# Feed-forward weights at 64, 96 and 160 bytes from the input, modulo 256, instead of 32

## The chip, the core and the metric

The kernel runs on one core of a Trainium2 chip (trn2). The metric is the device time of one execution in microseconds (us); the time before is the median of three runs. One further execution was taken with the hardware profiler; its lines are what this document quotes. In them PE is TensorE (matmuls), PEld is its loading of weights, DVE is VectorE, ACT is ScalarE, POOL is GpSimd and SP is SyncE. L154 is line 154 of the kernel before.

## The reference

One block of a decoder on 512 positions of 1024 channels, in float32. The part that matters here is its second half, the feed-forward with a gate, whose 2816 inner channels pass a short causal convolution:

```python
x = x + mix @ w_o[l]
h = rmsnorm(x, norm2_g[l])
gu = h @ w_ffn_in[l]
g = causal_dwconv(gu[..., :D_FF], ffn_conv_w[l]) + ffn_conv_b[l]
x = x + (jax.nn.silu(g) * gu[..., D_FF:]) @ w_ffn_out[l]
```

Ahead of it stand the input projections, a sparse attention with three branches, a short convolution, two merge gates and the output projection `w_o`.

## The kernel before, in words

All activations lie with channels on the 128 partitions and positions along the row. Every float32 product is made of three matmuls in the type `float32r`: the operands are split into a high part and the rest, and high x high, high x low and low x high are summed in PSUM. `dense` (L149 to L162) issues them, one unit of three matmuls per 128 channels of the contraction: L154 (weights high, input high), L157 (weights high, input low), and L159 or, where all low weights come last, L161 (weights low, input high). Each matmul has its own load of 128 x 128 weights, and the load for the next one runs while the input of the present one streams.

The feed-forward input product `h @ w_ffn_in` is made by a fast matrix product with seven multiplications in place of eight. For two tiles of 128 output channels (`f`, `f + 1`), `n` = 0 (gate) or 1 (up), the weights form a 2 x 2 block matrix, of which seven blocks or sums of blocks ("forms") are needed, and likewise seven sums of the input, which are made once. There are 11 values of `f` and 2 of `n`, so 22 passes. The forms are:

- `a11` and `a12`, in the tiles `wh` and `wl` (`form_a1`, L956). For a few passes the low part is made by a DMA that adds, in tile `dl` (`lo_by_dma`, L967).
- 3 and 2, a pair: one tile `sh` (high) and one `sl` (low) of 2 x 512 columns each; and 4 and 1, a second pair in tiles of the same kind (`forms_s`, L976). DVE makes the sums (L991 to L996), and `put` (L982) splits them with one ACT and one DVE instruction. The tags `sh` and `sl` have four buffers each (`NSQ`), used in turn: the pairs of two passes.
- `a22`, in the tiles `th` and `tl` (`form_a22`, L999).

The input's sums lie in `xf_h` and `xf_l` (L1061, L1062), four tiles of channels by seven sums by 256 columns: two halves of the 512 positions. `ff_pair` (L1127) issues the seven products of a pass, each over four tiles of channels with 256 columns streaming, 12 matmuls a product. Between passes stand down products (`down_products`, L1210), 512 columns wide, whose weights are in `wh`, `wl` or `dl`; the last few are 256 wide.

Where a tile lies in a partition's memory is decided by pools. `px` and `pf` lie on the left side, one behind the other; `pw`, with the pairs and `a22`, grows from the right end downward, and so does `pc` below it, which holds `mix_h` and `mix_l`, the input of the `w_o` product (L1089 to L1101; 8 output tiles of 24 matmuls, 512 columns wide). Padding tiles fix the addresses: `xf_pad` of `XF_PAD` = 8 words ahead of `xf_h`, and `pf_pad` of `PF_PAD` = 48 words, which brings what follows in `pf` back to its place. The addresses of the built program, modulo 256 bytes, are: the parts of `wh`, `wl`, `dl` that hold weights, `sh`, `sl`, `th`, `tl`, `ah`, `al`, `mix_h` and `mix_l` at 224, `xf_h` and `xf_l` at 0. So the feed-forward weights lie 32 bytes ahead of (below) their input, and the weights of the down products and of `w_o` at the same place as theirs.

In the token projection (`tok_products`, L235, and `first_products`, L252) roles are different: the activations `xg_h` and `xg_l` are the loaded operand, at 224, and chunks of 350, 350 and 348 columns of weights (`th`, `wh_t`, `tok_lo`) stream from many different addresses. In the attention's scores (L732, L733) the keys `kk` stream, from 224 or 96, and the queries `qT`, at 224 or 96 too, are loaded.

The order of all instructions is fixed by a scheduler when the program is built.

Of the kernel before, what the change touches and what calls it, by code (L numbers as in the profile page):

```python
# [11 lines left out]
F32 = mybir.dt.float32  # L12
F32R = mybir.dt.float32r
# [5 lines left out]
P = 128  # L19
# [22 lines left out]
C_G = C_V + 256  # L42
TOKC = C_G + 24
LINE = 256
XF_PAD = 8
PF_PAD = 48
NW4 = 5
NWR = 3
NE = 3
# [15 lines left out]
NSQ = 4  # L65
# [29 lines left out]
def tile_block(ctx: ExitStack, tc: tile.TileContext, xT, pos, par, par2, w_tok, w_a3, w_gate, w_ao, w_bo, w_o,  # L95
# [12 lines left out]
    def const(shape, name, dt=F32, pool=sb):  # L108
        return pool.tile(shape, dt, name=name, tag=name)
# [827 lines left out]
    pw = ctx.enter_context(tc.tile_pool(name="pw", bufs=1, side="right"))  # L937
# [8 lines left out]
    def split(h, l, v):  # L946
        m = nc.scalar.activation(h, v, AF.Copy)  # L947
        nc.vector.tensor_sub(l, v, h.bitcast(F32))  # L948
        return m
# [17 lines left out]
    def lo_by_dma(name, raw, src, view=lambda t: t, after=None):  # L967
# [5 lines left out]
        nc.gpsimd.dma_start(view(l), src, accum_op=ALU.add)  # L973
        return l

    def forms_s(f, n, raws, form):  # L976
        nm = f"{n}_{f}"
        a11, a12 = raws[0][:, 0:half], raws[0][:, half:D]
        a21, a22 = raws[1][:, 0:half], raws[1][:, half:D]
        q = lambda name, tag, dt, bufs: pw.tile([P, 2, half], dt, name=f"{name}{nm}", tag=tag, bufs=bufs)  # L980

        def put(names, v):  # L982
            h, l = (q(f"s{x}{names[0]}", f"s{x}", F32R, NSQ) for x in "hl")
            m = split(h, l, v)
            if names[0] == 4:
                ends["sh"] = m
            for i, name in enumerate(names):
                form[name] = (h[:, i], l[:, i])

        s = q("s32", "sf", F32, NSF)  # L990
        nc.vector.tensor_sub(s[:, 0], a11, a21)  # L991
        nc.vector.tensor_sub(s[:, 1], a22, s[:, 0])  # L992
        put((3, 2), s)
        s4 = q("s41", "sf", F32, NSF)
        nc.vector.tensor_sub(s4[:, 0], a12, s[:, 1])
        nc.vector.tensor_add(s4[:, 1], a21, a22)  # L996
        put((4, 1), s4)
# [11 lines left out]
    def ff_forms(f, n):  # L1009

        form = {}
        raws = [ff_raw(f, n, m) for m in range(2)]
        form_a1(f, n, raws[0], form)
        forms_s(f, n, raws, form)
        form_a22(f, n, raws[1], form)
        return form
# [5 lines left out]
    def first_sums(n):  # L1022
        forms_s(0, n, [ff_raw(0, n, m) for m in range(2)], first_form[n])
# [35 lines left out]

    const([P, XF_PAD], "xf_pad", F32, px)  # L1060
    xf_h = const([P, 4, 7, TH], "xf_h", F32R, px)  # L1061
# [48 lines left out]
    for i in range(NU):  # L1110
        u = const([P, 2, S + 2], f"c{i}", F32, pf)
        nc.gpsimd.memset(u[:, :, 0:2], 0.0)
        u_bufs.append(u)
    const([P, PF_PAD], "pf_pad", F32, pf)
    a_hl = {}
# [196 lines left out]
```

## Time and profile before

| | |
|---|---|
| time, median of three runs | 716.25 us (716.16 to 717.05) |
| time of the profiled execution | 716.42 us |
| its span, first to last instruction | 714.5 us |
| PE busy | 709.0 us (99%) |
| PEld busy | 635.7 us (89%) |
| DVE busy | 574.1 us (80%) |
| ACT busy | 415.5 us (58%) |
| POOL busy | 127.3 us (18%) |
| matmuls in the trace | 4275 |

A matmul's row gives the time from its start to the modelled end of its result; successive matmuls overlap, so that the sum of durations is longer than the busy time of PE. What a matmul costs in a row of matmuls is the time from its start to the start of the next, called a step here. A group's row reads: line, engine, operation, out<-in, partitions x elements, count, then busy us and mean ns of one, then idle time ahead of it.

### The profile page before, as it was taken

The page shows a single profiled execution, that of the slowest core. Times are in us where ns is not written, and L with a number is a line of the kernel's source. Part 1 is how long each engine was busy: PE and PEld are TensorE (multiplying, and loading weights), DVE is VectorE, ACT ScalarE, POOL GpSimd, SP SyncE. Part 2 cuts the span into 40 slices and gives each one's busy share as a digit, 9 for nine tenths or more (in the row PEclk, how much of TensorE's full clock was granted, in tenths as well). Part 3 has the DMA queues.
Part 4 walks back from the last instruction along what each step waited for, and adds up shares of the span by engine and source line. Part 5 has one row for each costly group of instructions (what it writes and reads, how often), then busy time and mean ns, then how long its engine had stood idle before and what let it go on. Part 6 is the DMA issues. An engine that isn't in the chain of part 4 may idle for free.

```text
span 714.5 us, 11190 instructions
## 1 busy us (share of the span) xinstructions
PE 709.0 (99%) x4275; PEld 635.7 (89%) x4275; DVE 574.1 (80%) x988; ACT 415.5 (58%) x706; POOL 127.3 (18%) x111
## 2 busy tenths in 40 slices
PE   9999999999999999999999999999999999999997
PEld 8999888888888888888889999999999999999986
DVE  7978978785566784788876999899898998989833
ACT  7776566777767875444665665555455554455320
POOL 1122443343333311232002011010000010000000
PEclk9999999999999999999999999999999999999999
DMA  8633552121111122246447476645655556552413
GB/s 297 228 89 100 159 126 73 47 90 59 60 60 59 60 64 84 91 146 202 181 133 163 118 170 165 167 120 124 174 145 129 138 124 161 129 148 89 118 30 117
DMA packets 36804, 88.19 MB, mean 123 GB/s; under 512 B 7440, under 2 KB 10896, under 8 KB 36752
## 3 DMA queue, kind: packets, MB, share of 16 engines
q1 hardware_dynamic: 30672, 74.42, 32.8%
q0 software_dynamic: 5648, 12.58, 10.8%
q8 instruction: 33, 0.54, 0.3%
q10 hardware_dynamic: 432, 0.49, 0.2%
q14 instruction: 19, 0.16, 0.1%
HBM read 85.39 MB, written 2.10 MB: 122 GB/s over the span
## 4 chain that ended last, share of the span: by engine, by line
PE 92%; issue 4%; DMA 2%; DVE 1%; POOL 0%; ACT 0%; POOLq 0%; SPq 0%; DVEq 0%
PE p L154 8%; PE p L161 8%; PE p L157 8%; PE pdn L157 4%; PE pdn L154 4%; PE pg L159 4%; PE pg L157 4%; PE pg L154 4%; PE pdn L161 4%; PE pa L154 3%; PE pa L157 3%; PE pt L810 2%; PE po L161 2%; PE po L157 2%; PE po L154 2%
## 5 line engine op out<-in xcount | busy, mean ns | idle before, releaser
L154 PE MATMUL p<-xf_h,sh 128*128 128x256 f32 x352 | 86.4, 280 | 0.0
L157 PE MATMUL p<-xf_l,sh 128*128 128x256 f32 x352 | 86.0, 278 | 0.0
L154 PEld LDWEIGHTS p<-xf_h,sh 128*128 128x128 f32 x352 | 66.5, 189 | 0.1
L157 PEld LDWEIGHTS p<-xf_l,sh 128*128 128x128 f32 x352 | 65.9, 187 | 0.0
L947 ACT ACTIVATE sh<-s 128x1024 fp32r<-128x1024 f32 x44 | 45.7, 1050 | 19.0 <-DVE s L992 15.7
L973 POOL DMA_DIRECT2D wl_d<-in_w_dn_dram x16 | 19.1, 1195 | 204.0 <-ACT wl_d L970 204.0
L948 DVE TENSOR_TENSOR sl<-s,sh 128x1024 fp32r<-128x1024 f32 x44 | 53.1, 1216 | 2.8 <-ACT sh L947 2.7
L161 PE MATMUL p<-xf_h,sl 128*128 128x256 f32 x352 | 54.9, 279 | 0.0
L157 PE MATMUL pdn<-al,wh_d 128*128 128x512 f32 x134 | 52.4, 391 | 0.0
L154 PE MATMUL pdn<-ah,wh_d 128*128 128x512 f32 x134 | 52.0, 390 | 0.0
L159 PE MATMUL pg<-xg_h,wl_g 128*128 128x512 f32 x128 | 50.5, 395 | 0.0
L157 PE MATMUL pg<-xg_l,wh_g 128*128 128x512 f32 x128 | 50.3, 393 | 0.0
L154 PE MATMUL pg<-xg_h,wh_g 128*128 128x512 f32 x128 | 50.3, 393 | 0.0
L161 PEld LDWEIGHTS p<-xf_h,sl 128*128 128x128 f32 x352 | 47.4, 188 | 0.3
L154 PE MATMUL p<-xf_h,wh_s 128*128 128x256 f32 x176 | 43.3, 280 | 0.0
L157 PE MATMUL p<-xf_l,wh_s 128*128 128x256 f32 x176 | 43.1, 278 | 0.0
L761 ACT ACTIVATE e<-sc,mx 128x512 f32<-128x512 f32 (+3 forms) x64 | 33.2, 521 | 16.5 <-DVE mx L760 14.7
L154 PE MATMUL pa<-xg_h,wh_a 128*128 128x512 f32 x96 | 37.9, 395 | 0.0
L157 PE MATMUL pa<-xg_l,wh_a 128*128 128x512 f32 x96 | 37.6, 392 | 0.0
L787 ACT ACTIVATE e<-e,sums 128x512 f32<-128x512 f32 (+3 forms) x64 | 30.7, 552 | 8.2 <-DVE sums L737 8.0
L814 DVE TENSOR_TENSOR pl<-pt,ph 128x512 fp32r<-128x512 f32 x40 | 27.1, 683 | 10.2 <-ACT ph L813 10.0
L161 PE MATMUL pdn<-ah,wl_d 128*128 128x512 f32 x128 | 34.2, 389 | 0.0
(361 smaller groups left out, 2111.5 us busy)
## 6 DMA issues: line engine op xcount, KB each, us to landing
wr_s<-in_w_ff_dram SPq DMA_DIRECT2D x44, 512.0 KB, 3.8
wr_d<-in_w_dn_dram SPq DMA_DIRECT2D x22, 512.0 KB, 3.7
wr_g<-in_w_gate_dram SPq DMA_DIRECT2D x16, 512.0 KB, 3.5
wl_d<-in_w_dn_dram POOLq DMA_DIRECT2D x16, 512.0 KB, 6.6
wr_a<-in_w_a_dram SPq DMA_DIRECT2D x12, 512.0 KB, 3.7
wr_t<-in_w_tok_dram SPq DMA_DIRECT2D x10, 524.0 KB, 6.2
wr_o<-in_w_o_dram SPq DMA_DIRECT2D x8, 512.0 KB, 3.8
wr_ao<-in_w_ao_dram SPq DMA_DIRECT2D x4, 512.0 KB, 3.4
```

The source lines that it names most:

```text
L154: m = nc.tensor.matmul(acc, wh, xh, start=first and i == 0, stop=False)
L157: nc.tensor.matmul(acc, wh, xl, start=False, stop=False)
L159: m = nc.tensor.matmul(acc, wl, xh, start=False, stop=last and i == n - 1)
L161: m = nc.tensor.matmul(acc, wl, xh, start=False, stop=last and i == n - 1)
L761: nc.scalar.activation(e[:, i, 0:nk], sc[:, o:o + nk], AF.Exp, bias=mx[:, i], accum_out=sums[:, i])
L787: nc.scalar.activation(v, v, AF.Copy, scale=sums[:, i])
L810: ends["pt"] = nc.tensor.transpose(pt[:, i * P:(i + 1) * P], e[:, i, kt * P:(kt + 1) * P], ident)
L814: m = nc.vector.tensor_sub(pl, pt, ph.bitcast(F32))
L947: m = nc.scalar.activation(h, v, AF.Copy)
L948: nc.vector.tensor_sub(l, v, h.bitcast(F32))
L973: nc.gpsimd.dma_start(view(l), src, accum_op=ALU.add)
```

## The change

`XF_PAD` goes from 8 to 40 words, which moves `xf_h` and `xf_l` up by 128 bytes, and `PF_PAD` from 48 to 16, which keeps what follows in place. The tags `sh` and `sl` are divided into `sh3`, `sl3` (forms 3 and 2) and `sh4`, `sl4` (forms 4 and 1), with two buffers each instead of four for both. At the first use of each pair a padding tile is made: 56 words under the first pair's, 48 under the second's.

```diff
-XF_PAD = 8
-PF_PAD = 48
+XF_PAD = 40
+PF_PAD = 16
+S32_PAD, S41_PAD = 56, 48
...
+    pads = {3: [], 4: []}
+
     def forms_s(f, n, raws, form):
...
         def put(names, v):
-            h, l = (q(f"s{x}{names[0]}", f"s{x}", F32R, NSQ) for x in "hl")
+            h, l = (q(f"s{x}{names[0]}", f"s{x}{names[0]}", F32R, NSQ // 2) for x in "hl")
             m = split(h, l, v)
+            if not pads[names[0]]:
+                pads[names[0]].append(const([P, S32_PAD if names[0] == 3 else S41_PAD], f"pad{names[0]}", F32, pw))
```

The addresses of the built program, modulo 256 bytes, before and after:

| tiles | before | after |
|---|---|---|
| `xf_h`, `xf_l` | 0 | 128 |
| `sh`, `sl` of forms 3 and 2 | 224 | 64 |
| `sh`, `sl` of forms 4 and 1 | 224 | 32 |
| weights in `wh`, `wl`, `dl`, `th`, `tl` | 224 | 224 |
| `mix_h`, `mix_l` | 224 | 64 |
| `ah`, `al` | 224 | 224 |

Measured downward from the input, the weights are at 64 (forms 3, 2), 96 (forms 4, 1) and 160 bytes (`a11`, `a12`, `a22`).

## The prediction

> **What bounds the kernel now.** I read the page first, then the busy time by stretches, then the groups of matmuls by tile and shape, and last the timeline of single matmuls. The page:
>
> ```profile
> span 714.5 us, 11190 instructions
> ...
> PE 709.0 (99%) x4275; PEld 635.7 (89%) x4275; DVE 574.1 (80%) x988; ACT 415.5 (58%) x706; POOL 127.3 (18%) x111
> ...
> PE 92%; issue 4%; DMA 2%; DVE 1%; POOL 0%; ACT 0%; POOLq 0%; SPq 0%; DVEq 0%
> ```
>
> PE is busy for 709.0 of 714.5 us, and 92% of the chain that ended last is PE. So a nanosecond more or less on one matmul is a nanosecond of the kernel, as long as no other engine comes up behind it. The stretches show whether one does (first the stage of the output projection `w_o`, then the feed-forward):
>
> ```profile
> 328.70:372.30 43.60, 43.60 (x194) 36.15 (x193) 33.64 (x51) 27.24 (x40) 4.43 (x3) 1.00 0.56 175
> 372.30:677.60 305.30, 304.74 (x2244) 289.04 (x2244) 277.23 (x372) 162.49 (x203) 25.09 (x23) 1.00 0.56 139
> ```
>
> The columns are length, then busy time of PE, PEld, DVE, ACT and POOL, the granted clock, and the DMA share. In the feed-forward stretch PE has no idle time to speak of (304.74 of 305.30), the clock is 1.00, and DVE, which makes the weights' forms, has 277.23, so 28 us of slack. A gain of a few us on PE stays covered.
>
> **The unit of the sum: one 256-wide step.** In each pass of the feed-forward (22 of them) the seven products have 4 units of 3 matmuls, 84 in all: 24 with forms 3 and 2, 24 with forms 4 and 1, 36 with the other three. That is 528, 528 and 792, together 1848. One pass in the timeline, its first row and the first row after it:
>
> ```profile
> 612.24 0.28 PE L154 MATMUL p<-xf_h,wh_s 128*128 128x256 f32 x1
> ...
> 622.04 0.39 PE L154 MATMUL pdn<-ah,wh_d 128*128 128x512 f32 x1
> ```
>
> (622.04 - 612.24) / 84 = 116.7 ns from start to start; 1848 such steps are 215.7 us. The pipelined matmul itself lasts longer; its duration by groups, here for a pair's high and low parts:
>
> ```profile
> L154 PE MATMUL p<-xf_h,sh 128*128 128x256 f32 x341 | 83.5, 280 | 0.0
> L157 PE MATMUL p<-xf_l,sh 128*128 128x256 f32 x341 | 83.3, 278 | 0.0
> L161 PE MATMUL p<-xf_h,sl 128*128 128x256 f32 x341 | 53.2, 279 | 0.0
> ```
>
> The mean is 279 ns, so step = duration - 162 ns. Durations can thus be compared where the timeline's 10 ns are too coarse.
>
> **The change, part by part.** It removes, adds and moves no instruction: rows and waits of all five engines are the same in both programs. Tiles `s`, `s4`, `sh`, `sl` still have as many buffers (two for each pair, taken in turn, as four taken in turn by two pairs gave), so no wait for a buffer changes. Only addresses change. I call "ahead" the input's address minus that of the weights loaded while it streams, modulo 256 bytes. It goes from 32 everywhere to 64 (forms 3, 2), 96 (forms 4, 1) and 160 (the others). One thing moves that the change doesn't speak of: `mix_h` and `mix_l`, which lie below the pair tiles, go from 224 to 64 modulo 256, and the 192 matmuls of `w_o` (8 tiles of 24) from 0 to 96 ahead (64 - 224 is -160, or 96 modulo 256).
>
> Does the distance cost anything? Before has other distances in other places. Distance 0, at the same width of 256, in the last down products:
>
> ```profile
> L157 PE MATMUL pdn_e<-al,wh_d 128*128 128x256 f32 x12 | 3.3, 283 | 0.0
> L154 PE MATMUL pdn_e<-ah,wh_d 128*128 128x256 f32 x12 | 3.3, 282 | 0.0
> L159 PE MATMUL pdn_e<-ah,wl_d 128*128 128x256 f32 x12 | 3.2, 282 | 0.0
> ...
> 698.03 0.28 PE L157 MATMUL pdn_e<-al,wh_d 128*128 128x256 f32 x1
> ...
> 698.87 0.28 PE L154 MATMUL pdn_e<-ah,wh_d 128*128 128x256 f32 x1
> ```
>
> Seven steps in 0.84 us are 120 ns, 3.3 more than at 32 ahead, and the durations say the same (282 to 283 against 279). Distance 128, width 256, in two score products of the attention, each a pair of rows:
>
> ```profile
> L732 PE MATMUL sc<-kk,qT 128*128 128x256 f32 x1 | 0.3, 279 | 0.0
> L733 PE MATMUL sc<-kk,qT 128*128 128x256 f32 x1 | 0.3, 279 | 0.0
> ...
> L733 PE MATMUL sc<-kk,qT 128*128 128x256 f32 x1 | 0.3, 282 | 0.0
> L732 PE MATMUL sc<-kk,qT 128*128 128x256 f32 x1 | 0.3, 276 | 0.0
> ```
>
> Mean 279, as at 32 ahead; 276 is the shortest that I find at this width. The new distances themselves occur only in the token projection, where 350 columns stream. There, pairs of matmuls on one chunk of weights, two pairs each in the order 0 ahead, 32 ahead, 160 ahead, 96 ahead:
>
> ```profile
> L242 PE MATMUL pj_t<-wh_t,xg_l 128*128 128x350 f32 x1 | 0.3, 323 | 0.0
> L239 PE MATMUL pj_t<-wh_t,xg_h 128*128 128x350 f32 x1 | 0.3, 322 | 0.0
> L239 PE MATMUL pj_s<-wh_t,xg_h 128*128 128x350 f32 x1 | 0.3, 323 | 0.0
> L242 PE MATMUL pj_s<-wh_t,xg_l 128*128 128x350 f32 x1 | 0.3, 318 | 0.0
> ...
> L239 PE MATMUL pj_t<-th,xg_h 128*128 128x350 f32 x1 | 0.3, 322 | 0.0
> L242 PE MATMUL pj_t<-th,xg_l 128*128 128x350 f32 x1 | 0.3, 321 | 0.0
> L239 PE MATMUL pj_s<-th,xg_h 128*128 128x350 f32 x1 | 0.3, 320 | 0.0
> L242 PE MATMUL pj_s<-th,xg_l 128*128 128x350 f32 x1 | 0.3, 320 | 0.0
> ...
> L242 PE MATMUL pj_s<-wh_t,xg_l 128*128 128x350 f32 x1 | 0.3, 326 | 0.0
> L239 PE MATMUL pj_s<-wh_t,xg_h 128*128 128x350 f32 x1 | 0.3, 321 | 0.0
> L239 PE MATMUL pj_t<-wh_t,xg_h 128*128 128x350 f32 x1 | 0.3, 325 | 0.0
> L242 PE MATMUL pj_t<-wh_t,xg_l 128*128 128x350 f32 x1 | 0.3, 323 | 0.0
> ...
> L242 PE MATMUL pj_t<-th,xg_l 128*128 128x350 f32 x1 | 0.3, 327 | 0.0
> L239 PE MATMUL pj_t<-th,xg_h 128*128 128x350 f32 x1 | 0.3, 322 | 0.0
> L239 PE MATMUL pj_s<-th,xg_h 128*128 128x350 f32 x1 | 0.3, 322 | 0.0
> L242 PE MATMUL pj_s<-th,xg_l 128*128 128x350 f32 x1 | 0.3, 322 | 0.0
> ```
>
> Means 321.5, 320.75, 323.75 and 323.25. So at this width 160 ahead costs 3.0 ns over 32 ahead, and 96 ahead 2.5. But 0 and 32 differ by less than 1 ns there, against 3.5 at width 256: where 350 columns stream the distance acts otherwise, and a row of the same width counts more for me.
>
> Term by term, from rows of width 256 first:
> - Forms 3 and 2, 64 ahead. From 0 to 32 bytes the duration fell by 3.5 ns. Another 32 bytes on the same slope go to the shortest row, 276, that is -3 ns. Bounds: -3 (that row) and +3.5 (the row at 0). I take -3: 528 x -3 = -1.6 us.
> - Forms 4 and 1, 96 ahead. Between 64 ahead (-3 by the slope) and 128 ahead (0 by the score rows); the token rows say +2.5. Bounds -3 and +3.5. I take half the gain, -1.5: 528 x -1.5 = -0.8 us.
> - Other forms, 160 ahead. The nearest row of the width is 128 ahead, 279: nothing. The token rows say +3. Bounds -3 and +3.5. I take 0.
> - `w_o`, 0 to 96 ahead, width 512:
>
> ```profile
> L154 PE MATMUL po<-mix_h,wh_o 128*128 128x512 f32 x64 | 24.7, 389 | 0.0
> ```
>
> No row of this width shows another distance within one stage. The token rows give 323.25 - 321.5 = +1.75 from 0 to 96; the bounds are -3.5 (what 0 to 32 gave at width 256) and +3.5. I take +1.75: 192 x 1.75 = +0.3 us.
>
> Sum: -1.6 - 0.8 + 0 + 0.3 = -2.1 us. The profiled execution took 716.42 us (span 714.5 and 1.9 around it), the median of the runs is 716.25, so the two agree within 0.2. 716.4 - 2.1 = 714.3 us.
>
> A rule of the Trainium skill speaks against this change. The page "TensorE: Matmul & The Clock Gate", in "Step-by-step: what each phase is for", says that TensorE reads the streaming operand and the next weights through two independent ports, so that loading the next weights takes nothing from the running matmul. By that rule distance couldn't matter and the time would stay. The 282 to 283 ns against 279 of the same shape speak against it, unless something else than distance sets those rows apart. In its section "Back-to-back issue gap" the same page gives N / 2.4 + 2.5 ns, an estimate of 109.2 ns for 256 columns; by it 1848 steps could lose 13.9 us at most. No row here comes near: 276 ns is a step of 114.
>
> **The rivals.**
> - *Nothing happens.* The step of 116.7 ns is the same for all forms, and score rows half a period away have 279 as well. If this is a floor set by the alternation of load and matmul, with 0 the only bad distance, the three terms are 0 and `w_o` is left: 716.4 + 0.3 = 716.7 us. Against it speak the single durations of 276, below that floor. The rule of the two ports would give this case too.
> - *Slower.* What the token projection shows holds for 256 columns as well: 32 ahead is near the best place, and 96 and 160 ahead are near the worst. The place is the steps of forms 4, 1 and of the others: 528 x 2.5 + 792 x 3.0 = 1.3 + 2.4 = +3.7 us, nothing for 64 ahead, +0.3 for `w_o`: 720.4 us. It decides as soon as these 1320 steps lose about 0.8 ns each (1.1 us, which with the 0.3 of `w_o` is 0.2%). For it: these are the only rows with just these distances. Against it: their width, and the weak answer to 0.
> - *All three gain.* Everything but the surroundings of 0 reaches the shortest row: 1848 x -3 = -5.5, +0.3: 711.2 us. Against it: the score rows at 128, which don't reach it on the mean.
>
> **How the numbers follow.** Two measurements of this kernel differ by up to 0.2% (716.16 to 717.05 in three runs is 0.12%), so 1.4 us is what counts as a change. Chances: forecast 0.33, all three gain 0.14, nothing happens 0.26, slower 0.27. The first two are faster by over 0.2%: 0.47. Same 0.26, slower 0.27. The cases have both signs, and the likeliest has its own range: with each of its three terms off by 1 ns, 714.3 +- 1.8. The whole range reaches down past the case of all three (711.2, less 0.8) and up to the slower case (720.4), of which it keeps somewhat more than half; less than 2 in 10 lies outside: 710.4 to 720.6.
>
> **What would show it.** In the profile after, the groups of `p` by tile: `sh`, `sl` mix the two pairs, since the names carry no number there, but a stretch of the timeline within one product tells them apart. Right would be 276 for forms 3 and 2, 277 to 278 for 4 and 1, 279 for `wh_s`, `wl_s`, `th`, `tl`, and 391 in place of 389 for `po`. 279 everywhere is the first rival; 281 to 282 in `wh_s` and `th` the second. I am wrong altogether if the order on PE's chain changes, or if idle time appears before matmuls of `p`: then addresses moved more than the reads of PE. The weakest step is the slope from two points, 0 and 32.

## The result, and the profile after

The changed kernel takes 721.2 us (median of four runs, 720.64 to 722.03), the kernel before 716.24 us on the same chip. The ratio is 1.0066, 95% interval 1.0053 to 1.0079: slower by 5 us. The forecast was 714.3 us, with 720.6 as the upper end of the range. The second rival, "slower", gave 720.4.

The page of the changed kernel:

```profile
span 719.0 us, 11190 instructions
...
PE 713.3 (99%) x4275; PEld 637.8 (89%) x4275; DVE 574.5 (80%) x988; ACT 415.3 (58%) x706; POOL 124.6 (17%) x111
...
PE 96%; DMA 2%; ACT 1%; SPq 0%; DVE 0%; issue 0%
```

The span grew by 4.5 us (719.0 against 714.5) and the busy time of PE by 4.3 (713.3 against 709.0). No other engine moved by more than 3 us, the counts are the same, and PE is 96% of the chain. So nothing new is waited for: the same matmuls take longer. Three products show it. The busy time from 300 us to the end, each line for the instructions of one tile alone: first `p` (the feed-forward product), then `po` (the product with `w_o`), then `pdn` (the down products between the passes). The columns are length, then busy us and count of PE and PEld, then the other engines. Before:

```profile
300.00:714.50 414.50, 220.19 (x1848) 219.08 (x1848) 52.30 (x88) 8.31 (x22) 1.00 0.52 139
300.00:714.50 414.50, 43.81 (x192) 35.98 (x192) 5.49 (x8) 0.00 (x0) 1.00 0.52 139
300.00:714.50 414.50, 95.37 (x402) 73.97 (x402) 23.21 (x34) 1.00 0.52 139
```

After:

```profile
300.00:719.00 419.00, 222.72 (x1848) 221.82 (x1848) 52.25 (x88) 8.34 (x22) 1.00 0.51 137
300.00:719.00 419.00, 45.09 (x192) 35.97 (x192) 5.49 (x8) 0.00 (x0) 1.00 0.51 137
300.00:719.00 419.00, 95.74 (x402) 73.98 (x402) 23.12 (x34) 1.00 0.51 137
```

That is +2.5 us for `p`, +1.3 for `po` and +0.4 for `pdn`, together 4.2 of the 4.5 us. What is left over is nearly nothing: `w_o` starts 0.9 us later (329.6 against 328.7), and a wait of 0.6 us for the transfer of a `wl_s`, which the feed-forward of before has, doesn't occur after. The clock is 1.00 in all rows. The groups after, of which the prediction named the durations it expected:

```profile
L155 PE MATMUL p<-xf_h,sh 128*128 128x256 f32 x352 | 87.3, 281 | 0.0
L155 PE MATMUL p<-xf_h,wh_s 128*128 128x256 f32 x176 | 43.8, 281 | 0.0
L155 PE MATMUL po<-mix_h,wh_o 128*128 128x512 f32 x64 | 25.1, 395 | 0.0
L155 PE MATMUL p<-xf_h,th 128*128 128x256 f32 x88 | 21.7, 279 | 0.0
```

395 for `po` was 389, and 391 had been expected. `sh` mixes the two pairs. To take them apart I sorted the steps (start of one matmul to start of the next, waits left out) by the distance between the streaming input and the weights of the next matmul, which are loaded meanwhile. Mean steps of the feed-forward, in ns:

| forms | before, all 32 ahead | after | worth |
|---|---|---|---|
| 3 and 2 | 116.7 | 117.0 (64 ahead) | +0.3 x 525 = +0.1 us |
| 4 and 1 | 116.7 | 119.9 (96 ahead) | +3.2 x 524 = +1.7 us |
| `a11`, `a12`, `a22` | 116.8 | 118.0 (160 ahead) | +1.2 x 797 = +1.0 us |
| `w_o`, 512 wide | 226.7 (0 ahead) | 233.4 (96 ahead) | +6.7 x 191 = +1.3 us |

(The counts are the steps that could be told apart in the trace.) Start rows in the timeline of after, in the last two passes; each `sh` row is the first of 24 matmuls of a pair, in the order forms 2 and 3, then 4 and 1, and the `th` row is the first behind them:

```profile
665.19 0.28 PE L155 MATMUL p<-xf_h,sh 128*128 128x256 f32 x1
...
668.02 0.28 PE L155 MATMUL p<-xf_h,sh 128*128 128x256 f32 x1
...
670.90 0.28 PE L155 MATMUL p<-xf_h,th 128*128 128x256 f32 x1
...
675.12 0.28 PE L155 MATMUL p<-xf_h,sh 128*128 128x256 f32 x1
...
677.85 0.28 PE L155 MATMUL p<-xf_h,sh 128*128 128x256 f32 x1
...
680.72 0.28 PE L155 MATMUL p<-xf_h,th 128*128 128x256 f32 x1
```

Forms 4 and 1 take 2.88 and 2.87 us for 24 steps, 120 ns, in both passes. Forms 3 and 2 take 2.83 us in the first pass, 118 ns, but 2.73 us in the second, 113.8 ns. The same forms at the same distance thus have two values, and 113.8 is the gain of 3 ns that the prediction expected. Of the 20 passes in which the 24 matmuls of forms 3 and 2 stand in one piece, 4 have 113.7 to 113.8 and the others 117.8 to 118.0. These four (their pairs start at 398.34, 408.17, 417.99 and 675.12 us) follow another pass with no down product in between; so does one more, the second pass (388.42 us), which has 117.8. This oddity becomes the second question of the experiments.

### The profile page after: what moved, and what is told of

Its sections match the earlier page's. It is cut to its first block, busy times and chain, and to the rows that moved or that the text cites. A ratio compares the mean times of both kernels' runs of the same rounds, so it can differ in the third digit from the quotient of the medians.

```text
span 719.0 us, 11190 instructions
## 1 busy us (share of the span) xinstructions
PE 713.3 (99%) x4275; PEld 637.8 (89%) x4275; DVE 574.5 (80%) x988; ACT 415.3 (58%) x706; POOL 124.6 (17%) x111
## 4 chain that ended last, share of the span: by engine, by line
PE 96%; DMA 2%; ACT 1%; SPq 0%; DVE 0%; issue 0%
PE p L155 10%; PE p L158 10%; PE p L162 10%; PE pdn L155 4%; PE pdn L158 4%; PE pg L158 4%; PE pg L160 4%; PE pg L155 4%; PE pdn L162 4%; PE pa L155 3%; PE pa L158 3%; PE pt L811 2%; PE po L162 2%; PE po L155 2%; PE po L158 2%; PE pa L160 2%
```

## The experiments

**Theory D:** the distance modulo 256 between the streaming operand and the weights being loaded sets the step, by a curve that neither the slope from 0 to 32 nor the token projection's rows gave. **Rival A:** the change of the pair tiles or of other addresses acts otherwise (the tiles' own places, DVE or ACT on them), and distance is a bystander. All kernels keep the order of the matmuls and differ from before or after in addresses alone, except the last.

### The side move of `w_o` alone, and taken back

```diff
 mix_only (kernel before)            mix_back (kernel after)
     mix_l = const(...)                  mix_l = const(...)
+    const([P, 40], "mx_pad", F32, pc)  +    const([P, 24], "mx_pad", F32, pc)
```

`mix_only` puts `mix_h` and `mix_l` 96 bytes ahead in the kernel before; `mix_back` puts them back to 0 in the kernel after.

> The kernel before with a padding tile that moves mix_h and mix_l alone, by 160 bytes, so that only w_o goes from 0 to 96 ahead; the feed-forward stays at 32. Distance theory: w_o steps 233.4 ns, time 716.2 + 1.3 = 717.5. Rival, that the slow w_o steps came from the moved pair tiles above them: steps 226.7, time 716.2.

> The changed kernel with one more padding tile, which puts mix_h and mix_l back to 224 modulo 256, so that w_o is at distance 0 again; the feed-forward keeps 64, 96 and 160. If the 192 steps of w_o (233.4 ns after, 226.7 before) are a cost of the distance and stay on the path, they go back to 226.7 and the time falls by 192 x 6.7 = 1.3 us to 719.9. If that loss was hidden or is paid elsewhere, 721.2 stays.

Measured, as ratios to the time of before in the same series: `mix_only` 1.0015 (1.0006 to 1.0023), `mix_back` 1.0043 (1.0029 to 1.0057). The row of `po` in `mix_only`:

```profile
300.00:716.20 416.20, 45.10 (x192) 35.97 (x192) 5.50 (x8) 0.00 (x0) 1.00 0.50 138
```

And in `mix_back`:

```profile
300.00:717.40 417.40, 43.85 (x192) 35.97 (x192) 5.48 (x8) 0.00 (x0) 1.00 0.50 138
```

The 1.3 us come with the distance in one kernel and go with it in the other. They were a side effect of the pads, below the pair tiles, on a tile that the change doesn't name.

### The pairs and the others apart

`pairs_at_32` is the kernel after with both pairs 32 ahead and the other forms at 160; `pairs_only` leaves the others at 32 and has the pairs at 64 and 96. Both have `w_o` at 0.

```diff
 pairs_at_32 (kernel after)              pairs_only (kernel after)
-S32_PAD, S41_PAD = 56, 48              -XF_PAD = 40
+S32_PAD, S41_PAD = 0, 32               -PF_PAD = 16
-            if not pads[names[0]]:     +XF_PAD = 8
+            if not pads[names[0]] \    +PF_PAD = 48
+                    and names[0] == 4: -S32_PAD, S41_PAD = 56, 48
+    const([P, 32], "mx_pad", F32, pc)  +S32_PAD, S41_PAD = 56, 16
                                        +    const([P, 56], "mx_pad", F32, pc)
```

> The changed kernel with both pairs at 32 ahead of the input, which stays at its new address (128 modulo 256); the other forms stay at 160; mix is put back to distance 0. Distance theory: steps of the pairs 116.7 ns as before, others 118.0, time 716.2 + 797 x 1.3 = 717.2. Rival, that the input's own address of 128 modulo 256 makes the steps slow: pairs at the mean of after, 118 ns, like the others, time 716.2 + 1846 x 1.3 = 718.6.

> The changed kernel with the input back at its old address, so that the other forms are at 32 ahead again, the pairs still at 64 and 96, and w_o put back to distance 0. Distance theory, the parts add up: forms 3 and 2 at 117.0 to 117.6 ns (+0.2 to 0.5 us), forms 4 and 1 at 119.9 (528 x 3.2 = +1.7 us), others 116.7. Time 716.4 + 1.9 to 2.2 = 718.3 to 718.6. If forms 4 and 1 are slow for the input's address, 116.7 and 716.5.

Measured: `pairs_at_32` 1.0020 (1.0011 to 1.0029), `pairs_only` 1.0048 (1.0035 to 1.0061). The rows of `p`, first `pairs_at_32`:

```profile
300.00:715.60 415.60, 221.55 (x1848) 220.44 (x1848) 52.36 (x88) 8.36 (x22) 1.00 0.50 139
```

Then `pairs_only`:

```profile
300.00:716.10 416.10, 221.99 (x1848) 221.11 (x1848) 52.27 (x88) 8.33 (x22) 1.00 0.50 138
```

Against 220.19 of before that is +1.4 for the others at 160 and +1.8 for the pairs at 64 and 96, where the steps of after give 1.0 and 1.8. In `pairs_at_32` the input itself still lies at 128 modulo 256, and the pairs have 116.8 ns there, as before with the input at 0: it is the distance that counts, not the input's place. The time of `pairs_only` (719.4 us against 716.0) is 3.4 us above before, more than its `p` explains; 2.6 us of it are in the span (716.4 against 713.8, medians of the runs) and the rest in the time around the span, which was 2.5 us in its profiled execution against 1.9 in before's. I can't say why.

### The whole curve

Seven kernels have all forms at one distance (and `w_o` at another). They are the kernel before with another `XF_PAD` (16, 24, 32, 48, 56 words for 64, 96, 128, 192, 224 ahead), the rest of the 56 words in `PF_PAD`, and a pad behind `mix_l`. For 16 and 48 ahead, `xf_h` and `xf_l` are parts of one tile with an offset of 16 bytes; for `w_o` at 16 and 240, `mix_h` and `mix_l` likewise.

The edit of `all_64`:

```diff
-XF_PAD = 8
-PF_PAD = 48
+XF_PAD = 16
+PF_PAD = 40
...
     mix_l = const([P, KD, S], "mix_l", F32R, pc)
+    const([P, 56], "mx_pad", F32, pc)
```

> The kernel before with all feed-forward forms at 16 ahead and w_o at 64 ahead. If the step follows the distance smoothly, 16 lies between 0 (120.0 ns) and 32 (116.7): 118 ns; if addresses count in pieces of 32 bytes, 16 is like 0 (120) or like 32 (116.7). w_o: 233 ns if everything but 0 is equally bad at width 512 (32 and 96 were 233.3 and 233.4). Time: 716.2 + 1848 x 1.3 + 192 x 6.7 = 2.4 + 1.3, or 719.9; 721 to 724 if 16 is like 0.

> All feed-forward forms at 48 ahead, w_o at 160 ahead. Smooth curve: between 32 (116.7 ns) and 64 (117.0 to 117.6), so 117.1 and +0.7 us; if the lowest place lies between 32 and 64, less than 116.7. w_o: 233 ns, +1.3 us. Time 718.2 by the smooth curve, under 717.5 if 48 is a better place than 32.

> The kernel before with the input moved to 32 modulo 256, all forms at 64 ahead, and mix moved so that w_o is at 32 ahead. Distance theory: every feed-forward step at 117.0 ns, as forms 3 and 2 had after (their weights were at 64, here they are at 224), +0.5 us. Rival, that the weights' or the input's own address sets the step: another number, 118 or more. w_o at 32: if what 0 to 32 did at width 256 holds, 223 ns and -0.6 us; if it climbs toward 96, 229 ns and +0.4 us. Time 716.1 to 717.1 by the distance theory, 718.5 or more by the rival.

> All feed-forward forms at 96 ahead with every weight at 224 modulo 256 (after, forms 4 and 1 had it with weights at 32). Distance theory: 119.9 ns in all forms, +5.9 us. Rival, that 119.9 came from the place of the weights of forms 4 and 1 at 32 or from their standing between products of other distances: less than 118.5 ns. w_o at 16 bytes on the other side (240): 233 ns and +1.3 us if only 0 is good, 228 and +0.3 if the bad stretch begins slowly. Time 723.4 by the distance theory, 720 or less by the rival.

> All feed-forward forms at 128 ahead, a distance that the feed-forward had not had. Smooth curve between 96 (119.9 ns) and 160 (118.0 to 118.3): 119.0, +4.3 us; the score rows of the attention that the prediction took (279 ns of duration) would give 116.7. w_o at 16 ahead: 233 ns or 229, +1.3 or +0.4 us. Time 721.8 by the smooth curve, 717.5 by the score rows.

> All feed-forward forms at 192 ahead, w_o at 224 ahead, the part of the circle of 256 bytes not yet tried. The distance alone sets the step; the curve so far at width 256 is 120, 118.6, 116.7, 118.4, 117.6, 120.0, 119.6, 118.1 ns at 0, 16, 32, 48, 64, 96, 128, 160. If 32 is the only low place, 118 to 119 here, +2.4 to 4.2 us; if there is a second low place opposite 64, 117 and +0.5. w_o at width 512: 233 ns (+1.3 us) if only 0 is good. Time 718 to 721.7.

> All feed-forward forms at 224 ahead (32 on the other side of 0), w_o at 192 ahead. If only the amount counted and not the side, 224 would be like 32: 116.7 ns, and 716.2 plus 1.3 for w_o, 717.5. If the side counts, since the load starts some ns behind the streaming, it is near 0 or above: 119 to 120, +4.2 to 6.1 us, 721.7 to 723.6 with w_o.

> All feed-forward forms at 192 ahead, w_o at distance 0 as before: the only distance but 32 at which the feed-forward lost nearly nothing (117.0 ns), and at which the down products between the passes had the shortest steps of all (227.2 ns against 227.8). Distance theory: 717.7 less the 1.3 of w_o, 716.4, the same as before within 0.2%. A kernel faster than before, under 715, would need steps below 116 ns, which no run had on the mean.

Mean steps, with 0 from the 35 last down products of before (256 wide), 32 from before, 160 from after, and 0 and 96 at 512 columns from `w_o` in before and after:

| ahead, bytes | 256 wide, ns | ratio of the kernel | `w_o` 512 wide, ns |
|---|---|---|---|
| 0 | 119.1 | | 226.7 |
| 16 | 118.6 | 1.0045 (1.0030 to 1.0060), `w_o` at 64 | 231.7 |
| 32 | 116.7 | | 233.3 |
| 48 | 118.4 | 1.0065 (1.0048 to 1.0081), `w_o` at 160 | |
| 64 | 117.6 | 1.0036 (1.0023 to 1.0048), `w_o` at 32 | 229.0 |
| 96 | 120.0 | 1.0100 (1.0085 to 1.0115), `w_o` at 240 | 233.4 |
| 128 | 119.6 | 1.0089 (1.0074 to 1.0104), `w_o` at 16 | |
| 160 | 118.0 | | 234.2 |
| 192 | 117.0 | 1.0026 (1.0014 to 1.0039), `w_o` at 224 | 233.3 |
| 224 | 118.3 | 1.0061 (1.0041 to 1.0081), `w_o` at 192 | 233.4 |
| 240 | | | 233.4 |

Behind the values at 96 and 192 in the left column stand these rows of `p`, of `all_96`:

```profile
300.00:722.00 422.00, 226.03 (x1848) 225.01 (x1848) 52.41 (x88) 8.36 (x22) 1.00 0.49 136
```

and of `all_192`, whose second line is `po`:

```profile
300.00:715.80 415.80, 220.77 (x1848) 219.63 (x1848) 52.29 (x88) 8.30 (x22) 1.00 0.50 138
300.00:715.80 415.80, 45.08 (x192) 35.99 (x192) 5.48 (x8) 0.00 (x0) 1.00 0.50 138
```

With `w_o` back at 0, `all_192_w_o_0` comes to 1.0017 (1.0007 to 1.0027), not to the 1.000 of its profiled span (714.3 against 714.5). The profiled executions were not the typical ones here: over all runs of the series the median span is 714.95 us, against 713.8 of before. Theory D holds for the mean step, and rival A falls: the cost goes with the distance whichever operand was moved, and DVE and ACT are as busy as before. The curve is neither a slope nor a valley: 32 and 192 are low, 64 next, 96 and 128 high, 16 and 48 both well above 32. At 512 columns only 0 is low. The places in after where one form follows another point to the weights of the *next* matmul as those whose distance counts: the 22 steps with own weights at 64 and the next at 96 are 120.6 ns long, and the 28 with own at 96 and next at 160 are 116.4, while within the runs 64, 96 and 160 have 117.0, 119.9 and 118.0. The first number fits 96 well; the second is clearly not that of 96, but not that of 160 either.

### Two values at one distance

The mean at 192, like that of forms 3 and 2 in the kernel after, hides two values. In `all_192_w_o_0`, a product of a pair ahead of the first down products, and one late in the feed-forward (start rows, 24 steps each):

```profile
414.69 0.28 PE L154 MATMUL p<-xf_h,sh 128*128 128x256 f32 x1
...
417.40 0.28 PE L154 MATMUL p<-xf_h,sh 128*128 128x256 f32 x1
...
632.69 0.28 PE L154 MATMUL p<-xf_h,sh 128*128 128x256 f32 x1
...
635.52 0.28 PE L154 MATMUL p<-xf_h,th 128*128 128x256 f32 x1
```

2.71 us is 113 ns a step, 2.83 us is 118. The switch comes at 418.31 us, where the first down products (0 ahead) stand in the middle of a product; what follows them has 118. **Theory P:** the step depends on what ran just before, and the down products at 0 ahead bring the long one. **Rival R:** any 512-wide products do, at whatever distance. Four kernels move the down products' input `ah`, `al` alone:

```diff
+        if f == 0:
+            const([P, 48], "a_pad", F32, pf)
         h, l = (pf.tile([P, 2, S], F32R, name=f"a{x}{f}", tag=f"a{x}", bufs=NA // 2) for x in "hl")
+        if f == 0:
+            const([P, 16], "a_pad2", F32, pf)
```

(48 and 16 words put them 192 ahead, 16 and 48 words 64, 32 and 32 words 128. Three are `all_192_w_o_0` otherwise, the fourth is the kernel after.)

> All forms 192 ahead and w_o at 0, as in the kernel of before with 192 and w_o 0 (profiled span 714.3 us), and now the down products' weights 192 ahead of their input too instead of 0. Why: at 192 ahead the feed-forward step has two values in one and the same trace, 113.3 ns until the first down products and 117.8 ns after them. Theory P (what ran before sets the value, and the down products at 0 ahead bring the slow one): with the down products at 192 the switch is gone, 113.3 in all passes, about -6.4 us of the 1848 steps; the down products, 512 wide, go from 227.2 to about 233.3 (what w_o had at 192), 510 x 6.1 = +3.1 us. Span about 711, ratio 0.995 to 0.997. Rival R (any run of 512-wide products brings the slow value, whatever its distance): 117.8 stays, span about 717.4, ratio 1.005 to 1.006.

> All forms 192 ahead, w_o at 0, down products 64 ahead, where w_o had 229.0 ns: +0.9 us on the 510 down products. Theory P with the switch due to distance 0 alone: 113.3 in all passes, span about 709, ratio 0.992 to 0.993. If a change of distance of any size brings the slow value (P in a narrower form: only the same distance keeps it), and by rival R too: 117.8, span about 715.2, ratio 1.002 to 1.003.

> All forms 192 ahead, w_o at 0, down products 128 ahead, a distance not yet seen at 512 columns; from its neighbours (229.0 at 64, 233.3 to 234.2 at 160 and 192) 231.5 +- 2.5, +1 to +3.4 us. Theory P with distance 0 alone to blame: 113.3 in all passes, span 709 to 711.5. Narrow P and rival R: 117.8, span 715.3 to 717.7.

> The changed kernel, with the down products 64 ahead instead of 0; w_o stays at 96. In the changed kernel forms 3 and 2, 64 ahead, have 113.8 ns in the passes that no down product precedes and 118.0 in the others, and a11, a12 (160 ahead) 117.2 and 118.9. Theory P with distance 0 to blame: 113.8 and 117.2 in all passes, about 17 passes x 24 x 4.2 = -1.7 us and 17 x 24 x 1.7 = -0.7 us, +0.6 for the down products (512 wide, from 228.5 to 229.0 and some): span about 717.2, ratio 1.003 to 1.004. Rival R: 118.0 and 118.9 as in the changed kernel, span about 719.5, ratio 1.007.

Measured: `ff192_down192` 0.9970 (0.9958 to 0.9981), `ff192_down128` 0.9970 (0.9959 to 0.9981), `ff192_down64` 1.0029 (1.0017 to 1.0040), `after_down64` 1.0068 (1.0051 to 1.0085). First `p`, then `pdn`. In `ff192_down192`:

```profile
300.00:711.00 411.00, 214.49 (x1848) 213.54 (x1848) 52.20 (x88) 8.29 (x22) 1.00 0.50 140
300.00:711.00 411.00, 97.42 (x402) 73.97 (x402) 23.09 (x34) 1.00 0.50 140
```

In `ff192_down128`:

```profile
300.00:712.40 412.40, 214.43 (x1848) 213.47 (x1848) 52.27 (x88) 8.28 (x22) 1.00 0.51 140
300.00:712.40 412.40, 97.52 (x402) 73.92 (x402) 23.14 (x34) 1.00 0.51 140
```

In `ff192_down64`:

```profile
300.00:716.00 416.00, 220.53 (x1848) 219.46 (x1848) 52.31 (x88) 8.29 (x22) 1.00 0.50 138
300.00:716.00 416.00, 96.08 (x402) 73.99 (x402) 23.18 (x34) 1.00 0.50 138
```

In `after_down64`:

```profile
300.00:718.40 418.40, 222.67 (x1848) 221.76 (x1848) 52.26 (x88) 8.31 (x22) 1.00 0.49 138
300.00:718.40 418.40, 95.99 (x402) 74.07 (x402) 23.11 (x34) 1.00 0.49 138
```

With the down products at 192 or at 128, `p` falls by 6.0 us (220.53 of `all_192_w_o_0` to 214.5), and the same product that took 2.83 us above takes 2.72 in the trace of `ff192_down192`:

```profile
629.71 0.28 PE L154 MATMUL p<-xf_h,sh 128*128 128x256 f32 x1
...
632.43 0.28 PE L154 MATMUL p<-xf_h,th 128*128 128x256 f32 x1
```

Behind nearly every run of down products there the first step is 118 and the following 83 are 113 or 114; only early on, behind one short run (450.2 us), do 20 steps stay at 118. With 64, nothing changes: 220.53 as at 0. So rival R is wrong: down products 512 wide don't bring the long step by themselves. Theory P is right that what ran before decides, wrong in blaming 0 alone (64 does the same), and its narrow form, in which only the same distance keeps the short step, is wrong too (128 keeps it).

For the changed kernel this decides nothing. There the down products at 64 leave `p` where it was (222.67 against 222.72), but at 192 ahead 64 brought the long step just as 0 did, so `after_down64` doesn't test Theory P; down products at 128 or 192 would have, and were not run. It has one effect: of the four passes with the short step, the last (674.27 us here) has 117.8. And `pairs_only` shows that down products at 0 do not always bring the long step at 64 ahead. Right behind 12 of them, the 24 steps of forms 3 and 2 take 2.73 us, 113.8 ns each:

```profile
445.96 1.09 PE L162 MATMUL pdn<-ah,wl_d 128*128 128x512 f32 x4
446.89 0.28 PE L155 MATMUL p<-xf_h,sh 128*128 128x256 f32 x1
...
449.62 0.28 PE L155 MATMUL p<-xf_h,sh 128*128 128x256 f32 x1
```

Its last pass, with no down product ahead, has 118. What decides at 64 ahead is open.

At 192 and 128 the down products themselves lose 2.4 to 2.5 us against 95.05 in `all_192_w_o_0`, since 512 columns are at their best at 0 only. The last kernel makes each of the 402 down products between the passes of two that are 256 wide, in otherwise `ff192_down192`:

```diff
-                dense(acc, [(h[:, c], l[:, c], *(v[:, t] for v in a_hl[f0 + k])) for k, c in enumerate(cols)],
-                      first=not (held and last), last=not held or last, lo_last=not accs)
+                for t2 in ((slice(0, TH), slice(TH, S)) if accs == () else (t,)):
+                    dense(acc[:, t2.start - t.start:t2.stop - t.start],
+                          [(h[:, c], l[:, c], *(v[:, t2] for v in a_hl[f0 + k])) for k, c in enumerate(cols)],
+                          first=not (held and last), last=not held or last, lo_last=not accs)
```

> All forms and the down products 192 ahead, w_o at 0, as in ff192_down192 (profiled span 711.0 us), and the 402 down products between the passes, 512 wide, each made of two products 256 wide (804 with a load of weights each; the sums, the additions into x and the work of the other engines stay). Theory P (at 192 ahead and 256 wide a step of 113.4 ns keeps itself as long as nothing of another distance or width runs between): 804 x 113.4 = 91.2 us in place of 402 x 233.1 = 93.7, so -2.5 us; the 58 steps of 118 ns that followed the 512-wide products go as well (-0.3): span about 708.2, ratio 0.992 to 0.994. Rival R (a change of the loaded block's or the input's place brings the slow value by itself, or the fast one is kept only in a product's own run): the 2652 steps are at 117.8 at least in part, up to +10 us, ratio above 1.000.

Measured: 0.9987 (0.9953 to 1.0020), not told from no change. Its rows of `p` and `pdn`:

```profile
300.00:710.80 410.80, 214.41 (x1848) 211.76 (x1848) 52.66 (x88) 8.20 (x22) 1.00 0.51 140
300.00:710.80 410.80, 94.66 (x786) 91.77 (x786) 23.18 (x34) 1.00 0.51 140
```

(786 are 768 halves and 18 that stayed whole; 384 of the 402 were divided.) `pdn` fell by 2.8 us (97.42 to 94.66) as expected, and `p` stayed short. But the span is 710.8 against 711.0: of the 2.8 us about 1.1 went into a longer wait in the feed-forward (1.5 us for the transfer of a `wl_s`, where the other had 0.4 us for a `wh_s`) and 0.5 into the first 100 us (PE busy 98.48 against 98.93); the rest I haven't placed. The runs of this kernel fall into two groups, eight at 711.4 to 713.9 us and four at 720.9 to 724.6. The 9 us between their medians (712.6 and 721.7) are what some 2600 steps would lose between 113.4 and 117, which would fit a long step that keeps itself through a whole execution; no profile of such a run was taken, so this is only argued. The best versions measured are therefore `ff192_down192` and `ff192_down128`, both 0.9970 of before.

## Why the prediction was wrong

The step that failed is the price of a distance. The sum took the feed-forward's new distances for gains or for nothing (-1.6, -0.8 and 0 us), read off a line through two points, 0 and 32, and off score rows at 128. Measured by their steps they are +0.1, +1.7 and +1.0 us, since the step doesn't follow a line. `w_o` had the right sign, but a quarter of its size.

**Right.** The bound: no instruction moved, no wait replaced the gain or loss, and PE's time went to the end of the kernel nearly one for one (4.2 of 4.5 us). That distance matters, so "nothing happens" is refuted. That `mix_h` and `mix_l` move, and that it costs. The second rival had the place right: forms 4 and 1 and the others lose, forms 3 and 2 do not.

**Forms 3 and 2, "another 32 bytes on the same slope" (-3 ns, -1.6 us): wrong on the mean, +0.3 ns.** Two points were taken for a line, which the prediction itself named its weakest step. The next point on that line, 48 ahead, is at 118.4 ns. The point at 0 was off as well: it was read from seven steps of 120 ns and from durations, while all 35 steps of these products have 119.1 on the mean, 2.4 above 32 ahead and not 3.3 to 3.5. And 276 is not the shortest row: one score matmul, at 224.63 us, has 274. The value of -3 exists: 113.8 ns in four passes. In the other passes the step is 118. The down products decide which one comes at 192 ahead; what decides in the changed kernel stayed open, since the one kernel that moved them there (to 64) could not tell.

**Forms 4 and 1, "half the gain" (-1.5 ns, -0.8 us): measured +3.2 ns, +1.7 us.** The value was interpolated between the failed slope and score rows at 128. All kernels with 96 ahead agree, 119.7 to 120.0. The token rows, set aside for their width, had said +2.5.

**The others, "the nearest row of the width is 128 ahead, 279: nothing": measured +1.2 ns, +1.0 us.** The row was no good stand-in, for two reasons. 160 isn't 128 (118.0 against 119.6 ns), and two pairs of score matmuls could not stand for 128: a whole feed-forward at 128 has 119.6, 2.9 above 32 ahead. Here the token rows had said +3.0, too much.

**`w_o`, "+1.75 from 0 to 96" (+0.3 us): measured +6.7 ns, +1.3 us.** The mechanism was right and the size came from rows 350 columns wide. The bounds (-3.5, +3.5) came from 256 columns and didn't hold the value: at 512 columns every other distance measured costs 2.3 to 7.5 ns over 0. The prediction says that no row of this width shows another distance within one stage, and that is not so. Score products 512 wide stand at 0 and at 128 ahead (by the addresses of the built program): from one to the next it takes 227.8 ns on the mean of nine steps at 0, and 232.5 of six at 128, waits left out. These rows, for another distance, would have warned of about +5 ns.

Not foreseen: +0.4 us on the down products, whose distance did not change (step 227.8 before, 228.5 after). In the kernels with all forms at one distance it is 227.2 to 228.5, so it depends on the feed-forward's layout as well; that fits the finding that a step depends on what ran before, but no run isolates it.

The sum, as measured: +0.1 + 1.7 + 1.0 + 1.3 + 0.4 = 4.5 us, against -2.1. (The steps give 2.8 us for `p`, the busy rows 2.5.) The slower rival's +3.7 + 0.3 = +4.0 was nearly right by two errors that cancel: too much for 160 (3.0 for 1.2 ns, 1.4 us) and too little for 96 and `w_o` (0.4 and 1.0).

The rule that was weighed, from the Trainium skill's page "TensorE: Matmul & The Clock Gate", section "Step-by-step: what each phase is for" (the streaming read and the next weights' read have ports of their own, so the load takes nothing from the running matmul), would have given no change. It doesn't hold for this kernel: 116.7 against 120.0 ns at 256 columns and 226.7 against 233.4 at 512, with nothing but addresses changed. The estimate of 109.2 ns from the same page's "Back-to-back issue gap" was not reached at any distance; the shortest run of steps has 113.3. The Trainium skill gives that formula, in the same section, for an isolated matmul and says that in a stream of loads and matmuls both set the spacing. So it was no bound for this kernel to begin with.

## What to carry to other kernels

Where TensorE is the bound and each matmul has its own load of weights, as here, the place of a tile is a parameter like its size: write down, for each product, the distance modulo 256 bytes between the streaming operand and the weights loaded meanwhile, and measure the candidates at the very width, since 256 and 512 columns had different best distances. After a pad is put in, list every tile whose address moved: here more than a quarter of the loss (1.3 of 4.5 us) came from one that the change didn't mention. And when two points are all there is of a curve, take the bounds from them, not a slope; a few rows at another width warned better than the line did.

## What was not expected of the hardware

- The step at 256 columns has no simple dependence on the distance: 119.1, 118.6, 116.7, 118.4, 117.6, 120.0, 119.6, 118.0, 117.0, 118.3 ns at 0, 16, 32, 48, 64, 96, 128, 160, 192, 224. What makes 32 and 192 low is open.
- At 192 ahead (and, in after and `pairs_only`, at 64) the step is 113.3 to 113.8 or 117.8 to 118.0. At 192 what ran before decides: products 0 or 64 ahead in between leave the long one, products 128 or 192 ahead the short one. At 64 what decides is not known. Other distances have smaller pairs: 117.2 and 118.9 at 160 in after, 118.7 and 120.0 at 128. At 32 and 96 ahead with all forms there a single value was seen throughout (116.7 and 120.0). Why is open.
- The time outside the profiled span was 1.9 to 3.2 us among the profiled executions, and part of some differences of 0.1 to 0.2% lies there.
